# Moving a fold's first copy and addition into the list of woven jobs, and starting a unit's accumulating transfer ahead of its other half

## The chip, the cores and the metric

The kernel runs on one core of a Trainium2 chip. Its engines work in parallel, each on its own row of instructions: PE (TensorE, matrix products), DVE (VectorE), ACT (ScalarE), POOL (GpSimd) and SP (SyncE, which issues most transfers). The metric is the device time of one execution in microseconds (us), lower is better; the time before is the median of 3 runs, 2228.59 us (2227.19 to 2228.78).

## The reference

A decoder layer over 256 tokens of width 2048, all in float32: a half SwiGLU feed-forward (called f1 in the kernel), two gated token mixers (retention and windowed attention), a mixing projection, a second half feed-forward (f2) and a gated embedding, with a layer norm after each. Cut to what the change touches:

```python
def swiglu(x, w_gu, w_down):
    g, u = jnp.split(x @ w_gu, 2, axis=-1)
    return (jax.nn.silu(g) * u) @ w_down
...
h = layer_norm(alpha * h + 0.5 * swiglu(h, w_ffn1_gu[i], w_ffn1_down[i]), ln_g[i, 0], ln_b[i, 0])
...
rq, rk, rv, rg, aq, ak, av, gate_r, gate_a = jnp.split(h @ w_in[i], SPLIT_POINTS, axis=-1)
...
ret_branch = (jax.nn.silu(rg) * ro) @ w_ret_out[i]
...
mixed = (jax.nn.sigmoid(gate_r) * ret_branch + jax.nn.sigmoid(gate_a) * att_branch) @ w_mix_out[i]
...
h = layer_norm(alpha * h + 0.5 * swiglu(h, w_ffn2_gu[i], w_ffn2_down[i]), ln_g[i, 2], ln_b[i, 2])
```

The hidden width of the feed-forwards is 5632, so each has a gate/up product (2048 to 2 x 5632) and a down product (5632 to 2048).

## The kernel before, in words

**Split products.** A float32 weight tile w is split into a high part (a cast, ACT) and a low part w - high (a subtraction, DVE). PE makes three products for each pair of parts: lines L510, L511 and L512. Weights come in chunks of 512 KB, loaded by SP (L127), and are named by use: rf_gu is a raw chunk, hf_gu its high part, lf_gu its low part.

**Units.** The order of the weights is a plan, a list of units that are taken one after another. A `Single` is one chunk: cast L162 on ACT, subtraction L164 on DVE. A `Seven` holds two chunks and trades eight block products for seven (Strassen's way, in Winograd's form): DVE forms sums of blocks (L279, L280, L285, L289), ACT casts (L277, L278, L284, L293), DVE subtracts (L287, L294, L296, L298). A unit of kind "F" has a `Single` for one half and, for the other half, a pair `Folding` and `Folded`, which take the low part off DVE: ACT writes the rounded -raw into the low tile (L181), POOL issues a transfer that adds the raw chunk to it (L182), so that raw minus its rounding is left, and `Folded` casts the high part (L198). `fold_at` (L201) puts the `Folding` into the plan so many units ahead as `FOLD_AHEAD` says: 34 units of time for the first gate/up (f1_gu), 12 for the down products, 0 for the second gate/up (f2_gu).

**Buffers.** All these chunks and parts share a ring of 46 buffers of one size, which `slot` hands out in the order in which the program asks. `fill` loads from the plan and makes units as room allows; `done` frees a unit's room and calls `fill`, so the next unit's weights are made (`make_next`) while PE works on others.

**Stages and folds.** A gate/up has 11 stages, 0 to 10, one for each group of columns over the whole depth; stages 1 to 10 run as a `block` and end in a fold, named after the feed-forward and the stage (f12 is the fold of stage 2 of the first, f210 that of stage 10 of the second). Sums that only `Seven` units share stand in four extra banks, p1, p6, p7 and q5 (tiles f12s, mr0s and so on, after the block's name). When the last `Seven` of a block is done, its seven products run in the order p1, q5, p6, p7 and the rest, and `fold` combines the banks. `seven_common` does what all folds share: e = copy of p1 (ACT, L634), w0 = e + p6 (DVE, L635), w1 = w0 + p7 (L637), z = q5 - w (L639). The first two were issued at once, the others put into `woven`, a list of jobs: each call of `weave()` issues the next one, and the making of weights calls it between its own instructions. `idle` is an empty job. After the common part, a gate/up stage adds its own banks (L1105 to L1108, on f2g and f2u, f1g and f1u; a product at L1101), turns the result (ACT L227, a transposing transfer by SP, L231, ACT L238) and a mixer's block its two (L1669 to L1672). There are 28 folds: ten in each gate/up, two in each down product (f1d, f2d), two at the gates (ga0, ga1) and two at the retention output (mr0, mr1).

**Mixers.** Behind a fold of mr0 or mr1, DVE multiplies with the gates (sig, L1711) and adds (L1712), ACT writes the halves of the words (wmx, L227), SP turns them (mmx, L231), ACT joins (mixr, L238) and casts (mixt, L113), DVE subtracts (L114), and then the mixing projection can use it. The weights of the retention output (rw_ret, hw_ret, lw_ret) are made between these.

DVE, ACT and SP each take their instructions in the order in which they are written; that order, not a scheduler, decides what waits behind what.

Of the kernel before, what the change touches and what calls it, by code (L numbers as in the profile page):

```python
# [13 lines left out]
ALU = mybir.AluOpType  # L14
# [56 lines left out]
def layer(ctx: ExitStack, tc: tile.TileContext, io):  # L71
    nc = tc.nc
    sync, act, dve, pool, pe = nc.sync, nc.scalar, nc.vector, nc.gpsimd, nc.tensor
# [8 lines left out]
    def bank(name):  # L82
        return psum.tile([P, 512], F32, tag="ps", name=name)
# [4 lines left out]
    def slot(shape, dt, name):  # L88
        return slots.tile(shape, dt, tag="slot", name=name)
# [6 lines left out]
    plan = []  # L96
# [104 lines left out]
    def fold_at(ahead, key):  # L201

        begun = Folding(key)
        at, time = len(plan), 0
        while at > 0 and time < ahead:
            at -= 1
            time += plan[at].time
        if ahead and any(isinstance(u, Seven) for u in plan[at - 12 : at + 1]):
            while not isinstance(plan[at], Seven):
                at -= 1  # L210
        plan.insert(at, begun)
        plan.append(Folded(begun))

    class Turn:
# [92 lines left out]
    def weave_all():  # L307
        while woven:
            woven.pop(0)()
# [84 lines left out]
    def fill(must=False):  # L394

        while True:
            queued = sum(u.time for u in ready)
            left = room["slots"] - room["used"]
            wanted = must and not ready or not room["quiet"] and queued < room["ahead"]
            if loaded and wanted and loaded[0].makes <= left:  # L400
                make_next()
                continue
            first = loaded[0] if loaded else plan[0] if plan else None
            queued += sum(u.time for u in loaded)
            if plan and queued < room["far"] and plan[0].loads + first.makes <= left:
                u = plan.pop(0)
                u.load()
                room["used"] += u.loads
                loaded.append(u)
                continue  # L410
            return
# [9 lines left out]
    def take(key):  # L421
        while not ready:
            fill(True)
        u = ready.pop(0)
        assert u.key == key, (u.key, key)
        return u

    def done(u):
        room["used"] -= u.keeps
        fill()  # L430
        room["woven"] = room["woven"] + 1 if woven else 0
        if room["woven"] > 2:
            weave_all()
# [9 lines left out]
    idle = lambda: None  # L443

    def run_side(n=1):
        for _ in range(n):
            if side:
                side.pop(0)()
        for jobs in (slow, lazy):
            if jobs and next(jobs[0], "end") == "end":  # L450
                jobs.pop(0)
# [62 lines left out]
    def half_of(a, t):  # L514
        return tuple(x[:, t * P : (t + 1) * P] for x in a)

    def tokens_chunk(chunk, k0, lhs, sums, ts, kks=(0, 1)):
        for kk in kks:
            for t in ts:
                sums[t].add(half_of(lhs(k0 + kk), t), chunk.columns(kk))  # L520
# [11 lines left out]
    def block_units(units, keys):  # L532

        for kind, p in units:
            if kind == "P":
                plan.extend(Single(keys(n, p)) for n in range(2))
            elif kind == "F":
                plan.append(Single(keys(0, p)))
                fold_at(FOLD_AHEAD[keys(1, p)[0]], keys(1, p))
            else:  # L540
                plan.append((Seven if kind == "S" else Prepared)(keys(0, p), keys(1, p)))

    def block(name, units, keys, lhs, forms, sums, fold, before=None):


        sevens = [p for kind, p in units if kind in "SD"]
        extra = []
        for j, (kind, p) in enumerate(units):
            if before is not None:
                before(j)  # L550
            if kind in "PF":
                for n in range(2):
                    u = take(keys(n, p))
                    tokens_chunk(u.chunk, 2 * p, lhs, [sums[t][n] for t in range(2)], (0, 1))
                    done(u)
                    run_side()
                continue
            u = take(keys(0, p))
            weave_all()
            if not extra:  # L560
                extra = [Sum(bank(f"{name}s{j}"), len(sevens)) for j in range(4)]
            p1, p6, p7, q5 = extra
            a11, a12 = (half_of(lhs(2 * p + e), 0) for e in range(2))
            a22 = half_of(lhs(2 * p + 1), 1)
            f5, f6, f7, f3 = forms(p)
            q2, q3, q4 = sums[0][0], sums[0][1], sums[1][0]
            steps = [
                (p1, a11, u.b11), (q2, a12, u.b21), (q3, f3, u.b22), (q5, f5, u.t1),
                (p7, f7, u.t3), (p6, f6, u.t2), (q4, a22, u.t4),
            ]  # L570
            if p == sevens[-1]:
                steps = [steps[j] for j in (0, 3, 5, 4, 1, 2, 6)]
            for to, left, right in steps:
                to.add(left, right)
            done(u)
            run_side()
            if p == sevens[-1]:
                fold(p1.ap, p6.ap, p7.ap, q5.ap)

    def forms_sums(full):  # L580

# [49 lines left out]
    def seven_common(p1, p6, p7, q5):  # L631

        e, w, z = (slot([P, 2, 512], F32, n) for n in ("eve", "evw", "evz"))
        act.copy(e[:, 0], p1)  # L634
        dve.tensor_tensor(w[:, 0], e[:, 0], p6, ALU.add)  # L635
        woven.extend((
            lambda: dve.tensor_tensor(w[:, 1], w[:, 0], p7, ALU.add),  # L637
            idle,
            lambda: dve.tensor_tensor(z, q5[:, None, :].broadcast_to([P, 2, 512]), w, ALU.subtract),  # L639
        ))  # L640
        return e, w, z
# [423 lines left out]
    def ffn(name, i, ht, norm, keep, residual, keepers, away):  # L1065
# [60 lines left out]
        for j in range(KF // 4):  # L1126
# [22 lines left out]
            def before(u, j=j, offset=KD // 2 - len(units)):  # L1149
# [19 lines left out]
                if j == KF // 4 - 1 and u in (4, 6):  # L1169
                    convert(u // 2 - 2)  # L1170

            block(f"{name}{j}", units, gu_keys(name, j), rhs, forms, sums, lambda *a: got.extend(seven_common(*a)), before)
            if got:
                weave_all()
# [25 lines left out]
        def fold(b):  # L1200
            def f(*a):
                e, w, z = seven_common(*a)

                def scaled(x, v):
                    dve.scalar_tensor_tensor(x, x, 2.0 * ALPHA, v, ALU.mult, ALU.add)

                woven.extend((
                    lambda: scaled(y[2 * b][:, 0], e[:, 0]),
                    lambda: scaled(y[2 * b][:, 1], w[:, 1]),
                    lambda: scaled(y[2 * b + 1], z),  # L1210
                ))
            return f
# [25 lines left out]
        pn = [banks(f"{name}d{n}") for n in range(2)]  # L1238
        sums = [[Sum(pn[n][t], n_of[0][t, n]) for n in range(2)] for t in range(2)]
        block(f"{name}d0", first, down_keys(name, 0), lhs, forms, sums, fold(0), before_unit)  # L1240
        weave_all()
        for n in range(2):
# [21 lines left out]
        pt_ = [banks(f"{name}e{t}") for t in range(2)]  # L1264
        sums = [[Sum(pt_[t][n], n_of[1][t, n]) for n in range(2)] for t in range(2)]
        block(f"{name}d1", second, down_keys(name, 1), lhs, forms, sums, fold(1), before_unit)
        weave_all()
        slots_for_weights(27, last_ahead, last_ahead + 24)
# [72 lines left out]
    def mixers(ht, norm, residual, keepers, away):  # L1341
# [320 lines left out]
        def mixer_block(name, units, keys, lhs):  # L1662

            ps = [banks(name + w) for w in "ab"]
            got = []
            block(name, units, keys, lhs, forms, block_sums(ps, units, KD), lambda *a: got.extend(seven_common(*a)))
            weave_all()
            e, w, z = got
            dve.tensor_tensor(e[:, 0], e[:, 0], ps[0][0], ALU.add)  # L1669
            dve.tensor_tensor(e[:, 1], w[:, 1], ps[1][0], ALU.add)  # L1670
            for t in range(2):
                dve.tensor_tensor(z[:, t], z[:, t], ps[t][1], ALU.add)  # L1672
            return [e, z]
# [400 lines left out]
```

## Time and profile before

| | us |
|---|---|
| median of 3 runs | 2228.59 |
| profiled execution, its time | 2229.62 |
| its span in the profile | 2227.6 |
| DVE busy in it | 2011.8 |
| ACT busy in it | 1451.7 |
| transfers from HBM over the span | 490.20 MB, 235 GB/s |

The profiled execution is 1.03 us slower than the median. A row of the timeline reads: start, duration, engine, line, operation, output<-inputs, shape, count, and in brackets the idle time of the engine before it and what released it. The windows give for stretches of the span the busy time of each engine, then the granted clock of PE as a share (1.00 is all), the share of the transfer engines and GB/s. A window is cut at the end of p1, so it holds one stage from fold to fold. "x3" in a row are three instructions back to back.

### The profile page before, as it was taken

The numbers are of one execution on the slowest core, as the hardware profiler recorded it, in microseconds if no ns is written. First come the engines' busy times: TensorE is split into PE (matmuls) and PEld (weight loads), VectorE is DVE, ScalarE is ACT, GpSimd is POOL, SyncE is SP. The second block draws the span as 40 slices with busy tenths as digits, with TensorE's granted clock in tenths as the row PEclk, the third lists the DMA queues.
The fourth block names the chain that finished last, engine by engine and source line by source line (L and its number), as shares of the span: only waits on it lengthen the run. The fifth ranks groups of instructions, "written<-read, shape, count | busy, mean of one in ns | idle before, by whom it ended". The sixth has DMA issues, their size and how long they took to land.

```text
span 2227.6 us, 29127 instructions
## 1 busy us (share of the span) xinstructions
PE 2215.5 (99%) x10116; PEld 1832.7 (82%) x10116; DVE 2011.8 (90%) x2656; ACT 1451.7 (65%) x1691; POOL 48.4 (2%) x62
## 2 busy tenths in 40 slices
PE   9999999999999999999999999999999999999998
PEld 7788888888888888888788888888888877888887
DVE  5999999999988889889999888779999999899887
ACT  5877777777565545557866567466767678665553
POOL 0000000000000000000000000000000000000000
PEclk9999999999999999999999999999999999999999
DMA  9979889977686889846976578888899898777771
GB/s 315 259 227 264 249 241 263 255 239 235 225 301 238 296 280 331 274 171 228 293 232 232 174 216 323 306 302 269 290 313 312 292 265 260 215 242 234 283 290 69
DMA packets 303339, 573.91 MB, mean 258 GB/s; under 512 B 98764, under 2 KB 103756, under 8 KB 303192
## 3 DMA queue, kind: packets, MB, share of 16 engines
q1 hardware_dynamic: 293576, 541.70, 72.5%
q0 software_dynamic: 7632, 27.79, 6.7%
q10 hardware_dynamic: 1984, 2.58, 0.4%
q8 instruction: 79, 1.29, 0.2%
q14 instruction: 68, 0.56, 0.1%
HBM read 490.20 MB, written 33.55 MB: 235 GB/s over the span
## 4 chain that ended last, share of the span: by engine, by line
PE 92%; DMA 3%; DVE 3%; issue 2%; ACT 1%; SPq 0%; ACTq 0%; POOLq 0%; DVEq 0%
PE rqk L461 3%; PE f1g L512 3%; PE f1g L510 3%; PE f1g L511 3%; PE f2g L510 2%; PE f2g L511 2%; PE f2g L512 2%; PE f1u L512 2%; PE f1u L510 2%; PE f1u L511 2%; PE f2u L512 2%; PE f2u L510 2%; PE f2u L511 2%; PE aqk L461 2%; PE f2d L512 1%
## 5 line engine op out<-in xcount | busy, mean ns | idle before, releaser
L164 DVE TENSOR_TENSOR lw_in_f<-rw_in_f,hw_in_f 128x1024 fp32r<-128x1024 f32 x132 | 158.2, 1219 | 14.5 <-ACT hw_in_f L162 14.3
L164 DVE TENSOR_TENSOR lf_gu<-rf_gu,hf_gu 128x1024 fp32r<-128x1024 f32 x123 | 145.1, 1219 | 22.8 <-ACT hf_gu L162 22.1
L162 ACT CAST hf_gu<-rf_gu 128x1024 fp32r<-128x1024 f32 x123 | 123.3, 1048 | 29.7 <-DMA rf_gu<-in_f_gu 27.8
L293 ACT CAST hvf_gu<-vf_gu 128x1024 fp32r<-128x1024 f32 x83 | 87.5, 1055 | 76.5 <-DVE vf_gu L289 62.6
L284 ACT CAST huf_gu<-uf_gu 128x1024 fp32r<-128x1024 f32 x83 | 87.3, 1052 | 76.6 <-DVE uf_gu L280 69.3
L162 ACT CAST hw_in_f<-rw_in_f 128x1024 fp32r<-128x1024 f32 x132 | 132.5, 1049 | 6.9 <-DMA rw_in_f<-in_w_in_f 4.2
L164 DVE TENSOR_TENSOR lf_down<-rf_down,hf_down 128x1024 fp32r<-128x1024 f32 x96 | 115.6, 1220 | 20.5 <-ACT hf_down L162 16.3
L162 ACT CAST hf_down<-rf_down 128x1024 fp32r<-128x1024 f32 x96 | 98.5, 1049 | 27.3 <-DMA rf_down<-in_f_down 11.8
L287 DVE TENSOR_TENSOR lf_gu<-rf_gu,hf_gu 128x1024 fp32r<-128x1024 f32 x83 | 101.1, 1218 | 0.0
L298 DVE TENSOR_TENSOR lvf_gu<-vf_gu,hvf_gu 128x1024 fp32r<-128x1024 f32 x83 | 101.1, 1218 | 0.0
L296 DVE TENSOR_TENSOR luf_gu<-uf_gu,huf_gu 128x1024 fp32r<-128x1024 f32 x83 | 101.1, 1218 | 0.0
L277 ACT CAST hf_gu<-rf_gu 128x1024 fp32r<-128x1024 f32 x83 | 86.8, 1046 | 8.4 <-DMA rf_gu<-in_f_gu 8.4
L512 PE MATMUL f1g<-lf_gu,xt 128*128 128x512 f32 x223 | 87.1, 391 | 1.1 <-DVE lf_gu L164 1.1
L510 PE MATMUL f1g<-hf_gu,xt 128*128 128x512 f32 x223 | 87.0, 390 | 0.1
L511 PE MATMUL f1g<-hf_gu,xt 128*128 128x512 f32 x223 | 86.8, 389 | 0.0
L510 PE MATMUL f2g<-hf_gu,ht 128*128 128x512 f32 x196 | 76.4, 390 | 0.0
L512 PE MATMUL f2g<-lf_gu,ht 128*128 128x512 f32 x196 | 76.3, 389 | 0.0
L511 PE MATMUL f2g<-hf_gu,ht 128*128 128x512 f32 x196 | 76.3, 389 | 0.0
L512 PE MATMUL f1u<-lf_gu,xt 128*128 128x512 f32 x180 | 70.1, 390 | 0.0
L510 PE MATMUL f1u<-hf_gu,xt 128*128 128x512 f32 x180 | 70.1, 390 | 0.0
L511 PE MATMUL f1u<-hf_gu,xt 128*128 128x512 f32 x180 | 70.0, 389 | 0.0
L182 POOL DMA_DIRECT2D lf_gu<-rf_gu x37 | 32.2, 871 | 1636.9 <-DMA rf_gu<-in_f_gu 1105.6
(1568 smaller groups left out, 7220.3 us busy)
## 6 DMA issues: line engine op xcount, KB each, us to landing
rf_gu<-in_f_gu SPq DMA_DIRECT2D x362, 512.0 KB
rf_down<-in_f_down SPq DMA_DIRECT2D x176, 512.0 KB
rw_in_f<-in_w_in_f SPq DMA_DIRECT2D x148, 512.0 KB
lf_gu<-rf_gu POOLq DMA_DIRECT2D x37, 512.0 KB, 8.5
rw_rv<-in_w_rv SPq DMA_DIRECT2D x32, 512.0 KB
rw_ret<-in_w_ret SPq DMA_DIRECT2D x32, 512.0 KB
rw_mix<-in_w_mix SPq DMA_DIRECT2D x32, 512.0 KB
rw_pg<-in_w_pg SPq DMA_DIRECT2D x32, 512.0 KB
```

What stands on the lines that cost most here:

```text
L162: act.copy(c.hi, c.raw)
L164: dve.tensor_tensor(c.lo, c.raw, c.hi, ALU.subtract)
L277: act.copy(a.hi, a.raw)
L284: act.copy(uh, u)
L287: dve.tensor_tensor(a.lo, a.raw, a.hi, ALU.subtract)
L293: act.copy(vh, v)
L296: dve.tensor_tensor(ul, u, uh, ALU.subtract)
L298: dve.tensor_tensor(vl, v, vh, ALU.subtract)
L461: pe.matmul(ps[f], hi[:, kk, f * P : (f + 1) * P], rhs(k), start=k == 0, stop=k == n_k - 1,)
L510: pe.matmul(o, al, bh, start=first, stop=False)
L511: pe.matmul(o, ah, bh, start=False, stop=False)
L512: pe.matmul(o, ah, bl, start=False, stop=self.left == 0)
```

## The change

Three edits. In `fold_at`, where nothing is said to be ahead (f2_gu only), the `Folding` goes before the last unit of the plan, the `Single` of the same pair, and no longer after it. In `block`, the fold is called before the last unit's `done` and `run_side`. In `seven_common`, the copy and w0 are no longer issued at once but become the first job of `woven`, followed by an empty one; the other jobs move back by two. So the copy and w0 are issued in the first `weave()` of the next making, and their lines become one (L635; w1 is L637, z is L639).

```diff
-        plan.insert(at, begun)
+        plan.insert(at if ahead else len(plan) - 1, begun)
         plan.append(Folded(begun))
...
             for to, left, right in steps:
                 to.add(left, right)
+            if p == sevens[-1]:
+                fold(p1.ap, p6.ap, p7.ap, q5.ap)
             done(u)
             run_side()
-            if p == sevens[-1]:
-                fold(p1.ap, p6.ap, p7.ap, q5.ap)
...
         e, w, z = (slot([P, 2, 512], F32, n) for n in ("eve", "evw", "evz"))
-        act.copy(e[:, 0], p1)
-        dve.tensor_tensor(w[:, 0], e[:, 0], p6, ALU.add)
         woven.extend((
+            lambda: (act.copy(e[:, 0], p1), dve.tensor_tensor(w[:, 0], e[:, 0], p6, ALU.add)),
+            idle,
             lambda: dve.tensor_tensor(w[:, 1], w[:, 0], p7, ALU.add),
             idle,
             lambda: dve.tensor_tensor(z, q5[:, None, :].broadcast_to([P, 2, 512]), w, ALU.subtract),
```

The rows below are instructions as they stand on an engine; numbers behind a name are the buffer's count. First place: DVE at the fold f12 (end of stage 2 of the first gate/up, bank f12s), where the making of the next `Single`'s low part and the sums of the next `Seven` follow.

```order
 L164 TENSOR_TENSOR lf_gu_0_7_1110<-rf_gu_0_7_1011,hf_gu_0_7_1109 128x1024
 L164 TENSOR_TENSOR lf_gu_1_7_1135<-rf_gu_1_7_1057,hf_gu_1_7_1134 128x1024
-L164 TENSOR_TENSOR lf_gu_0_5_1166<-rf_gu_0_5_1095,hf_gu_0_5_1165 128x1024
 L635 TENSOR_TENSOR evw<-eve,f12s_985 128x512
+L164 TENSOR_TENSOR lf_gu_0_5_1169<-rf_gu_0_5_1095,hf_gu_0_5_1168 128x1024
 L279 TENSOR_TENSOR uf_gu_0_0_1195<-rf_gu_1_0_1142 128x512
 L280 TENSOR_TENSOR uf_gu_0_0_1195<-rf_gu_0_0_1140,rf_gu_1_0_1142 128x512
```

One subtraction, lf_gu_0_5, now stands behind w0 (L635) instead of ahead of it. Second place: DVE at the fold mr0 in the mixers (bank mr0s), up to z.

```order
 L164 TENSOR_TENSOR lw_ret_2_7_11889<-rw_ret_2_7_11850,hw_ret_2_7_11888 128x1024
-L164 TENSOR_TENSOR lw_ret_4_2_11914<-rw_ret_4_2_11852,hw_ret_4_2_11913 128x1024
-L164 TENSOR_TENSOR lw_ret_6_2_11918<-rw_ret_6_2_11854,hw_ret_6_2_11917 128x1024
 L635 TENSOR_TENSOR evw<-eve,mr0s_11641 128x512
-L279 TENSOR_TENSOR uw_ret_4_0_11942<-rw_ret_6_0_11874 128x512
-L280 TENSOR_TENSOR uw_ret_4_0_11942<-rw_ret_4_0_11872,rw_ret_6_0_11874 128x512
+L164 TENSOR_TENSOR lw_ret_4_2_11917<-rw_ret_4_2_11852,hw_ret_4_2_11916 128x1024
 L637 TENSOR_TENSOR evw<-evw,mr0s_11642 128x512
-L285 TENSOR_TENSOR vw_ret_4_0_11943<-rw_ret_4_0_11872,uw_ret_4_0_11942 128x512
-L287 TENSOR_TENSOR lw_ret_4_0_11946<-rw_ret_4_0_11872,hw_ret_4_0_11945 128x1024
+L164 TENSOR_TENSOR lw_ret_6_2_11923<-rw_ret_6_2_11854,hw_ret_6_2_11922 128x1024
```

Two subtractions, lw_ret_4_2 and lw_ret_6_2, go behind w0, with w1 (L637) between them; the sums of the next `Seven` (L279 on) follow after the second. At mr1 one subtraction goes behind w0 and one behind w1 in the same way, and on ACT the copy stands between the two casts that belong to them instead of behind both. Third place: ACT in the last stage of the second gate/up, at its last unit "F" (hf_gu and lf_gu ending in 0_6 and 1_6 are the two halves' parts).

```order
 L293 CAST hvf_gu_0_1_16884<-vf_gu_0_1_16868 128x1024
-L162 CAST hf_gu_0_6_16907<-rf_gu_0_6_16839 128x1024
-L181 ACTIVATE lf_gu_1_6_16942<-rf_gu_1_6_16853 128x1024
-L198 CAST hf_gu_1_6_16945<-rf_gu_1_6_16853 128x1024
+L181 ACTIVATE lf_gu_1_6_16907<-rf_gu_1_6_16839 128x1024
+L162 CAST hf_gu_0_6_16910<-rf_gu_0_6_16841 128x1024
+L198 CAST hf_gu_1_6_16945<-rf_gu_1_6_16839 128x1024
```

The start of the low part (L181) goes ahead of the other half's cast (L162); on SP the two loads rf_gu_0_6 and rf_gu_1_6 change places in the same way. There are ten such units in the second gate/up.

## The prediction

> **What bounds the kernel now.** I read the page first (span, busy time), then the waits of PE (TensorE), then the windows cut at the folds (the ends of the accumulations that the change touches), then the timelines around single folds.
>
> ```profile
> span 2227.6 us, 29127 instructions
> PE 2215.5 (99%) x10116; PEld 1832.7 (82%) x10116; DVE 2011.8 (90%) x2656; ACT 1451.7 (65%) x1691; POOL 48.4 (2%) x62
> ```
>
> PE is busy 2215.5 of 2227.6 us. So 12.1 us are left, and work on other engines counts only where it stops PE. PE's waits:
>
> ```profile
> PE f2u L512 <- DMA lf_gu<-rf_gu: 1.5, 2, 0.9
> PE f1g L512 <- DVE lf_gu L164: 1.1, 2, 0.5
> PE mr1a L512 <- DVE lw_ret L164: 0.5, 1, 0.5
> PE f29s L510 <- DVE evz L1108: 0.3, 1, 0.3
> ```
>
> The columns are total, times, longest. Three of these lie at places that the change touches: f2u (accumulating transfers of the second gate/up), mr1a (weights behind a fold), f29s (a bank that DVE empties). Matmuls start 0.23 us apart while each row lasts 0.39, so a pause that PE's rows show is a little shorter than the real one.
>
> Now the stages, cut where p1, the first bank of a fold, ends (columns: window, length, then busy PE, PEld, DVE, ACT, POOL):
>
> ```profile
> 125.50:165.60 40.10, 40.10 (x178) 33.21 (x178) 39.04 (x50) 29.29 (x33) 2.62 (x3) 1.00 0.75 219
> 206.50:246.60 40.10, 40.10 (x178) 33.20 (x178) 40.10 (x51) 29.76 (x33) 2.59 (x3) 1.00 0.84 244
> 287.70:327.80 40.10, 40.10 (x179) 33.20 (x178) 39.45 (x50) 29.29 (x32) 2.59 (x3) 1.00 0.76 226
> 1563.30:1602.70 39.40, 39.40 (x176) 32.62 (x175) 39.40 (x49) 27.11 (x30) 0.00 (x0) 1.00 0.83 283
> ```
>
> DVE (VectorE), not only PE, is full here: 40.10 of 40.10. In 125.50:165.60 it idles 1.06, in 287.70:327.80 it idles 0.65, each time in one wait that stands before the line that moves (below). How closely PE follows is seen at the ends of these stages:
>
> ```profile
> 165.25 1.21 DVE L298 TENSOR_TENSOR lvf_gu<-vf_gu,hvf_gu 128x1024 fp32r<-128x1024 f32 x1
> 246.46 1.22 DVE L298 TENSOR_TENSOR lvf_gu<-vf_gu,hvf_gu 128x1024 fp32r<-128x1024 f32 x1
> 327.18 1.22 DVE L298 TENSOR_TENSOR lvf_gu<-vf_gu,hvf_gu 128x1024 fp32r<-128x1024 f32 x1
> 166.57 0.45 PE L512 MATMUL f13s<-lvf_gu,f1fm 128*128 128x512 f32 x1
> 247.73 0.50 PE L512 MATMUL f15s<-lvf_gu,f1fm 128*128 128x512 f32 x1
> 328.80 0.39 PE L512 MATMUL f17s<-lvf_gu,f1fm 128*128 128x512 f32 x1
> ```
>
> The last weights are ready at 166.46, 247.68 and 328.40 and used at 166.57, 247.73 and 328.80: slack 0.11, 0.05 (the hand-off itself) and 0.40 us. A delay of DVE in these stages reaches PE almost whole.
>
> **The change, part by part.** No instruction is added or removed; all is order.
>
> *1. Copy and first addition into the list.* The addition w0 (L635) needs p1 and p6, and p6 ends later. It now stands ahead of one or two subtractions (L164) that are ready. DVE works in order, so when DVE is ahead of PE those queue behind a wait, and so does the next making of weights (L279 on). First gate/up stage:
>
> ```profile
> 122.76 3.49 DVE L164 TENSOR_TENSOR lf_gu<-rf_gu,hf_gu 128x1024 fp32r<-128x1024 f32 x3
> 127.31 0.69 DVE L635 TENSOR_TENSOR evw<-eve,f12s 128x512 f32<-128x512 f32 x1 [1.06 <-ACT lf_gu L181]
> 127.91 0.68 DVE L279 TENSOR_TENSOR uf_gu<-rf_gu 128x512 f32<-128x512 f32 x1
> 208.52 0.68 DVE L635 TENSOR_TENSOR evw<-eve,f14s 128x512 f32<-128x512 f32 x1
> 209.12 0.68 DVE L279 TENSOR_TENSOR uf_gu<-rf_gu 128x512 f32<-128x512 f32 x1
> 289.18 0.69 DVE L635 TENSOR_TENSOR evw<-eve,f16s 128x512 f32<-128x512 f32 x1 [0.65 <-PE f16s L512]
> 289.83 0.69 DVE L279 TENSOR_TENSOR uf_gu<-rf_gu 128x512 f32<-128x512 f32 x1
> ```
>
> At f16 w0 starts when PE lets it: 289.18, 1.48 after the cut at 287.70. Taken as the earliest w0 of every fold, this gives 126.98 (f12), 207.98 (f14). (At f12 it started 0.33 later than that, held by something of its tile's buffer; the tile gets another buffer now, so I drop that.) A subtraction takes (3.49-1.22)/2 = 1.135, an addition 0.60. So L279 comes at 126.98+0.60+1.135 = 128.71 instead of 127.91 (+0.80), at 207.98+1.735 = 209.71 instead of 209.12 (+0.59), and at 289.18+1.735 = 290.92 instead of 289.83 (+1.09). Less the slacks (0.05 being no slack): 0.80-0.06 = 0.74, 0.59, 1.09-0.35 = 0.74, together **+2.1**. These stages have no other DVE idle to absorb it; bounds 0 (if DVE catches up in ways the rows don't show) and +2.5 (no slack at all). In the stages between, and from f17 on, DVE is behind PE or waits for loads, and w0 finds its banks full: 0.
>
> *2. The same at the mixers' folds mr0 and mr1.*
>
> ```profile
> 1298.77 1.23 DVE L164 TENSOR_TENSOR lw_ret<-rw_ret,hw_ret 128x1024 fp32r<-128x1024 f32 x1 [0.63 <-ACT hw_ret L162]
> 1300.90 1.23 DVE L164 TENSOR_TENSOR lw_ret<-rw_ret,hw_ret 128x1024 fp32r<-128x1024 f32 x1 [0.90 <-ACT hw_ret L162]
> 1302.40 0.69 DVE L635 TENSOR_TENSOR evw<-eve,mr0s 128x512 f32<-128x512 f32 x1 [0.28 <-PE mr0s L512]
> 1311.17 0.68 DVE L1669 TENSOR_TENSOR eve<-eve,mr0a 128x512 f32<-128x512 f32 x1
> 1331.56 2.56 ACT L238 COPY mixr<-mmx 128x1024 uint16<-128x1024 uint16 x2 [0.63 <-DMA mmx<-wmx]
> 1335.20 1.99 ACT L162 CAST hw_ret<-rw_ret 128x1024 fp32r<-128x1024 f32 x2
> 1336.28 2.36 DVE L164 TENSOR_TENSOR lw_ret<-rw_ret,hw_ret 128x1024 fp32r<-128x1024 f32 x2 [0.18 <-ACT hw_ret L162]
> 1338.56 0.68 DVE L635 TENSOR_TENSOR evw<-eve,mr1s 128x512 f32<-128x512 f32 x1
> 1322.30 9.19 DMA mmx<-wmx
> ```
>
> Here w0 already waits for PE (0.28), until 1302.40, and both subtractions, done at 1298.77 and 1300.90 in the waiting time, now come after it: 2 x 1.135 = 2.27 later for L1669 and what follows. The chain of waits goes on from there without a break: DVE's sums, the transposing transfer mmx at 1322.30 (last row; 9.19 us), ACT's copies at 1331.56, casts at 1335.20, the subtraction at 1336.28, PE's wait at mr1a. All of it moves by +2.27, less nothing. At mr1 the copy (0.49) goes behind the first of the two casts, which ends at 1336.19, and w0 ahead of the subtraction that PE waits for: w0 at 1336.80, subtraction at 1337.40 instead of 1336.28, about +1.05. PE stands at that weight already, so the two add: **+3.3**. Bounds: +1.1 (the transfer's start is set by something else than DVE) and +3.8 (the 0.5 us of wait that PE has at mr1a now doesn't count against it).
>
> *3. The same in the second gate/up.*
>
> ```profile
> 1560.63 4.62 DVE L164 TENSOR_TENSOR lf_gu<-rf_gu,hf_gu 128x1024 fp32r<-128x1024 f32 x4
> 1565.17 0.68 DVE L635 TENSOR_TENSOR evw<-eve,f22s 128x512 f32<-128x512 f32 x1
> 1579.26 0.67 DVE L1108 TENSOR_TENSOR evz<-evz,f2u 128x512 f32<-128x512 f32 x1
> ```
>
> At f22 two of the four subtractions fall behind w0. DVE is through the other two at 1560.63+2x1.135 = 1562.90 and waits until 1563.30+1.48 = 1564.78: +1.88 for what follows. Weights are more than 3 us early there, so what matters is the bank that L1108 empties at 1579.93 and PE takes 1.6 us later: +0.3 to +0.4. f21 has the same +1.9 but no bank so near; f23 to f27 have 2 to 5 us of slack. f28 adds 0.2 before the full stage 9. Together **+0.6**, bounds 0 and +1.5 (the delays of f21, f24 and f29 reach PE by some tenths each).
>
> *4. The accumulating transfers one unit sooner.*
>
> ```profile
> 1867.39 1.04 ACT L162 CAST hf_gu<-rf_gu 128x1024 fp32r<-128x1024 f32 x1
> 1868.34 1.05 ACT L181 ACTIVATE lf_gu<-rf_gu 128x1024 fp32r<-128x1024 f32 x1
> 1869.75 0.86 POOL L182 DMA_DIRECT2D lf_gu<-rf_gu  x1 [17.54 <-ACT lf_gu L181]
> 1869.75 9.03 DMA lf_gu<-rf_gu
> ```
>
> L181 now comes ahead of the cast of its unit and its load ahead of the other half's load on SP's queue; nothing else on SP moves. ACT is free of waits here, so L181 is 0.95 sooner, or less if its load lands last: 0.3 to 0.95. The transfer of 9.03 us ends as much sooner, and PE's wait in stage 10 (the 0.9 among f2u's 1.5) shrinks by it: **-0.7**. In stage 9 the other 0.6 goes too, but at the stage's end PE meets DVE's last weights, as in 247.73 above, so it is worth 0. The cast of the unit comes 0.95 later, but DVE reaches its subtraction no sooner than before. Bounds -1.5 and +0.3 (DVE waits for the late cast).
>
> The 37 starts of these transfers on POOL (GpSimd) take this:
>
> ```profile
> L182 POOL DMA_DIRECT2D lf_gu<-rf_gu x37: 859/862/1020, 34.9 to 1869.8; - x37
> ```
>
> The Trainium skill (SBUF — State Buffer, A bandwidth-pool intuition that's wrong) has a case that speaks against part 4: while DVE holds the shared port, descriptors of a transfer issued from POOL can't be written, 620 ns becoming 3100 ns. The trace doesn't show it: 862 in the median and 1020 at most, beside a DVE that is full. By that rule the moved start could lose 2.5 us instead of gaining 0.7.
>
> *Earlier tiles.* The three tiles of the fold are taken earlier, so later loads get other buffers, some released up to 2 us later. Most of these loads wait for the queue and not for a buffer; I count 0, bounds 0 and +3 (the 2 us whole at one stage without slack, half at another).
>
> **Sum**: 2.1+3.3+0.6-0.7 = +5.3 us on the profiled execution, which took 2229.62 (2.0 around its span). The median of the runs shown, 2228.59, is 1.0 below it, so **2233.9**.
>
> **The rivals.**
> A. *What the change removes and no more.* If the waits at mr0, mr1 and f12 to f16 do not lengthen, f2u's 1.5, mr1a's 0.5 and f29s's 0.3 go, and with the start-to-start correction about 3.5: 2225.1. It decides where the banks are full before DVE comes to w0. The row at 208.52 speaks for it, where w0 waits for nothing; the 0.28 and 0.65 us of waits for PE before w0 in the rows above speak against it.
> B. *One of the two large terms is hidden:* the mixers (transfer not set by DVE) or the first stage: +5.3-2.1 or +5.3-2.2, 2231.9.
> C. *More than the sum:* loads into other buffers come late and DVE, full in most gate/up stages, can't make it up: +3 to +4 more, 2237.5.
> D. *POOL held at the moved start:* two subtractions of DVE, 2 x 1.135 = 2.27 us, less the 0.95 gained, make stages 9 and 10 each 1.3 later where the sum has 0.7 gained: 5.3+0.7+2.6 = +8.6, 2237.2. The 1020 ns above speak against it. This is the rule of the Trainium skill's page on SBUF, weighed in part 4.
> E. *The order changes and PE sees none of it:* 2228.6.
>
> **How the numbers follow.** Chances: forecast 0.46 (2231.5 to 2236.5 by its bounds), A 0.12, B 0.24, C 0.13, D 0.02, E 0.03. The range 2226.5 to 2238 leaves out most of A's lower part, and the top of C. A measurement tells 0.2% (4.5 us) from no change: faster is below 2224.1, slower above 2233.05. Slower has two thirds of the forecast, C and D: 0.47. Faster has the far half of A: 0.06. The rest is same: 0.47. The forecast stands just outside that bound.
>
> **What would show it.** Right: w0 preceded by a wait for PE of about 1.9 at f12, 1.3 at f14; L1669 2.3 later after mr0; PE's wait at mr1a 3 us longer; at 166, 247 and 328 PE pauses of 0.6 to 0.7 on L298. Part 4: POOL's start in stage 10 0.3 to 0.95 sooner against the cast L277 behind it, f2u's 1.5 near 0.5. Wrong: a total of PE's idle time under 12 us, mmx issued no later after mr0's p1, or pauses of PE on DMA at places that have none now (C).

## The result, and the profile after

The changed kernel takes 2232.92 us in the median of 13 runs (2230.79 to 2235.39), the kernel before 2227.31 us on the same chips (2225.64 to 2228.78). The ratio is 1.0024, 95% interval 1.0016 to 1.0033: slower by 0.24%, or 5.6 us. The forecast was 2233.9 against 2228.59, which is a ratio of 1.0024 too. The profiled execution took 2230.79 us.

The page of the profile after, span and busy time:

```profile
span 2229.0 us, 29129 instructions
PE 2215.6 (99%) x10116; PEld 1833.3 (82%) x10116; DVE 2009.9 (90%) x2656; ACT 1453.0 (65%) x1691; POOL 48.3 (2%) x62
```

The two spans differ by 1.4 us only, where the medians differ by 5.6. Most of the reason stands at the start. The copy at the fold f12 is a good clock for it, since it can't start before PE has filled its bank (timeline of ACT, before and then after; the row after names nothing that released it):

```profile
125.57 0.59 ACT L634 COPY eve<-f12s 128x512 f32<-128x512 f32 x1 [0.66 <-PE f12s L512]
```

```profile
122.01 0.59 ACT L635 COPY eve<-f12s 128x512 f32<-128x512 f32 x1 [1.80 <-issue]
```

The execution after reached f12 3.56 us sooner. Two more profiles of the kernel before (last two experiments) show that this start varies from run to run. So two single spans can hide a change of this size, and I compare stretches between the same instructions. PE's waits after (total, times, longest):

```profile
PE mr1a L512 <- DVE lw_ret L164: 2.4, 2, 1.6
...
PE f29s L512 <- DVE luf_gu L296: 0.7, 1, 0.7
PE f29s L510 <- DVE eve L1105: 0.3, 1, 0.3
PE f23s L510 <- DVE evz L1108: 0.3, 1, 0.3
PE f29s L510 <- DVE evz L1108: 0.3, 1, 0.3
```

mr1a went from 0.5 to 2.4, f23s is new, f2u's 1.5 is gone, and f29s has new waits of 0.7 for L296 and 0.3 for L1105. In the first gate/up, DVE around the folds f12, f14 and f16:

```profile
123.40 0.69 DVE L635 TENSOR_TENSOR evw<-eve,f12s 128x512 f32<-128x512 f32 x1 [2.03 <-PE f12s L512]
...
125.14 0.68 DVE L279 TENSOR_TENSOR uf_gu<-rf_gu 128x512 f32<-128x512 f32 x1
...
205.18 0.69 DVE L635 TENSOR_TENSOR evw<-eve,f14s 128x512 f32<-128x512 f32 x1 [1.08 <-ACT eve L635]
...
206.92 0.68 DVE L279 TENSOR_TENSOR uf_gu<-rf_gu 128x512 f32<-128x512 f32 x1
...
286.99 0.69 DVE L635 TENSOR_TENSOR evw<-eve,f16s 128x512 f32<-128x512 f32 x1 [1.71 <-PE f16s L512]
...
288.73 0.68 DVE L279 TENSOR_TENSOR uf_gu<-rf_gu 128x512 f32<-128x512 f32 x1
```

DVE now idles 2.03, 1.08 and 1.71 us before w0 (before: 1.06, 0 and 0.65), while the subtraction that stood ahead of w0 before now stands behind it. (The row at f14 names ACT's copy, but that ended at 204.35; the last product of p6 starts at 204.70 and its row ends at 205.09, so there too it is more likely PE that w0 waits for.) A stage later, PE at the last weights:

```profile
162.12 0.39 PE L511 MATMUL f13s<-huf_gu,f1fm 128*128 128x512 f32 x1
162.62 0.50 PE L512 MATMUL f13s<-luf_gu,f1fm 128*128 128x512 f32 x1
...
163.76 0.50 PE L512 MATMUL f13s<-lvf_gu,f1fm 128*128 128x512 f32 x1 [0.18 <-DVE lvf_gu L298]
...
245.53 0.50 PE L512 MATMUL f15s<-lvf_gu,f1fm 128*128 128x512 f32 x1 [0.17 <-DVE lvf_gu L298]
...
327.35 0.50 PE L512 MATMUL f17s<-lvf_gu,f1fm 128*128 128x512 f32 x1 [0.17 <-DVE lvf_gu L298]
```

The waits that the rows show are small (0.17), and 162.12 to 162.62 shows none at all, though matmuls that run freely start 0.23 apart: 0.27 is lost there. Only start-to-start times carry such pauses. From f12's copy to the first of these places PE takes 163.76-122.01 = 41.75 us (before 166.57-125.57 = 41.00), from there to the second 81.77 (before 247.73-166.57 = 81.16), to the third 81.82 (before 81.07): +0.75, +0.61, +0.75.

At the mixers, first the copy at mr0 and PE's wait in the timeline before:

```profile
1300.97 0.59 ACT L634 COPY eve<-mr0s 128x512 f32<-128x512 f32 x1
...
1337.56 0.50 PE L512 MATMUL mr1a<-lw_ret,rett 128*128 128x512 f32 x1 [0.53 <-DVE lw_ret L164]
```

Then the same and DVE between them, after (timelines of ACT, DVE and PE):

```profile
1299.61 0.59 ACT L635 COPY eve<-mr0s 128x512 f32<-128x512 f32 x1 [2.42 <-PE mr0s L512]
...
1301.04 0.69 DVE L635 TENSOR_TENSOR evw<-eve,mr0s 128x512 f32<-128x512 f32 x1 [4.10 <-PE mr0s L512]
...
1312.06 0.68 DVE L1669 TENSOR_TENSOR eve<-eve,mr0a 128x512 f32<-128x512 f32 x1
...
1337.42 0.69 DVE L635 TENSOR_TENSOR evw<-eve,mr1s 128x512 f32<-128x512 f32 x1 [0.65 <-ACT eve L635]
1338.03 1.22 DVE L164 TENSOR_TENSOR lw_ret<-rw_ret,hw_ret 128x1024 fp32r<-128x1024 f32 x1
...
1339.30 0.51 PE L512 MATMUL mr1a<-lw_ret,rett 128*128 128x512 f32 x1 [1.60 <-DVE lw_ret L164]
```

And the transposing transfer in the chain of waits after:

```profile
1323.18 8.97 DMA mmx<-wmx
```

Counted from the copy at mr0, L1669 comes after 12.45 us (before 10.20, +2.25), the transfer after 23.57 (before 21.33, +2.24), and the weight at mr1a after 39.69 (before 36.59, **+3.10**). DVE's idle 4.10 us before w0 holds what were two subtractions.

The parts of the span, all from rows shown here and in the prediction:

| stretch | before | after | difference |
|---|---|---|---|
| start to the copy at f12 | 125.57 | 122.01 | -3.56 |
| to the last weight at f17s | 203.23 | 205.34 | +2.11 |
| to the copy at mr0 | 972.17 | 972.26 | +0.09 |
| to the weight at mr1a | 36.59 | 39.69 | +3.10 |
| to the end of the span | 890.04 | 889.70 | -0.34 |

Without the start that is +5.0, beside 5.6 in the medians. How far each of these stretches varies from one run of a program to the next is shown with the last experiments.

### The profile page after: what moved, and what is told of

It reads as the page before. It is cut to its first block, busy times and chain, and to the rows that moved or that the text cites. A ratio compares the mean times of both kernels' runs of the same rounds, so it can differ in the third digit from the quotient of the medians.

```text
span 2229.0 us, 29129 instructions
## 1 busy us (share of the span) xinstructions
PE 2215.6 (99%) x10116; PEld 1833.3 (82%) x10116; DVE 2009.9 (90%) x2656; ACT 1453.0 (65%) x1691; POOL 48.3 (2%) x62
## 4 chain that ended last, share of the span: by engine, by line
PE 82%; DVE 4%; issue 1%; DMA 1%; ACT 0%; ACTq 0%; SPq 0%; DVEq 0%
PE rqk L461 3%; PE f2g L510 2%; PE f2g L511 2%; PE f2g L512 2%; PE f2u L510 2%; PE f2u L511 2%; PE f2u L512 2%; PE aqk L461 2%; PE f2e L512 1%; PE f2e L511 1%; PE f2d L512 1%; PE f1e L511 1%; PE f1d L512 1%; PE f1d L511 1%; PE f2d L511 1%; PE f1e L512 1%
## 5 line engine op out<-in xcount | busy, mean ns | idle before, releaser
L162 ACT CAST hw_in_f<-rw_in_f 128x1024 fp32r<-128x1024 f32 x132 | 132.6, 1048 | 6.7 <-DMA rw_in_f<-in_w_in_f 3.9
L162 ACT CAST hf_gu<-rf_gu 128x1024 fp32r<-128x1024 f32 x123 | 124.1, 1047 | 17.8 <-DMA rf_gu<-in_f_gu 17.8
L162 ACT CAST hf_down<-rf_down 128x1024 fp32r<-128x1024 f32 x96 | 98.6, 1049 | 29.5 <-DMA rf_down<-in_f_down 12.7
L298 DVE TENSOR_TENSOR lvf_gu<-vf_gu,hvf_gu 128x1024 fp32r<-128x1024 f32 x83 | 101.3, 1221 | 0.0
L296 DVE TENSOR_TENSOR luf_gu<-uf_gu,huf_gu 128x1024 fp32r<-128x1024 f32 x83 | 101.3, 1221 | 0.0
```

The costliest lines, as they stand in the source:

```text
L162: act.copy(c.hi, c.raw)
L296: dve.tensor_tensor(ul, u, uh, ALU.subtract)
L298: dve.tensor_tensor(vl, v, vh, ALU.subtract)
```

## The experiments

Each run was compared with the kernel before on the same chip; a figure in us is the difference of the two medians, and the interval is that of the ratio.

**The Folding's new place alone.**

```diff
-        plan.insert(at, begun)
+        plan.insert(at if ahead else len(plan) - 1, begun)
```

> Of the change only the Folding's place in the plan (part 4 of the prediction); copy and w0 as before. Theory (all of the loss comes from w0 waiting ahead of ready work on DVE): f1 and the mixers as before (PE's wait at mr1a 0.5), f2u's wait of 1.5 on the accumulating transfers gone, of which stage 9's part returns as a wait for DVE's last weights: 0.4 to 1.3 us less than before, most likely -1.0, within noise of no change. Rival (the changed order of loads and casts costs part of the loss): +1 us or more, with waits of PE in stages 4 to 10 of f2 that before doesn't have.

Measured: 2226.47 against 2226.44 us, ratio 0.9999 (0.9990 to 1.0008). A gain of 1 us is inside that interval and can't be told from it. In its profile f2u waits for no transfer, and PE's waits have this row, which no profile of the kernel before has:

```profile
PE f29s L512 <- DVE luf_gu L296: 0.7, 1, 0.7
```

The rival is not borne out: the profile has no other new wait in the second gate/up, though the interval alone would still allow +1 us. What the edit gains in stage 9 (0.75 us by start times) is given back at that stage's end (0.83), where PE, sooner there, waits for DVE.

**The list alone.** The change without the line above.

> Of the change only the copy and w0 in the list; the Folding's place as before. Theory: the whole loss and a little more, since the gain of the accumulating transfers is missing: +5.5 to +6.5 us, with PE waiting for L298 at the ends of f1's stages 3, 5 and 7 by 0.6 each, 2.4 in all at mr1a, 0.3 to 0.5 at f23s, and f2u's 1.5 still there. Rival (the loss hangs on both edits together): under +4.

Measured: 2232.41 against 2226.44 us, +6.0, ratio 1.0024 (1.0015 to 1.0033). mr1a has its 2.4 as expected, f23s 0.2 where 0.3 to 0.5 was expected, and from the copy at f12 to the last weight at f17s PE takes 205.28 us, as long as in the changed kernel (205.34). f2u is there:

```profile
PE f2u L512 <- DMA lf_gu<-rf_gu: 2.0, 2, 1.6
```

So the list carries the whole loss. In this profile 1.6 us behind the weight at mr1a is something else, told at the end (the clock).

**The whole change, with the mixers' two folds mr0 and mr1 as before.** A test of the block's name chooses between the fold ahead of `done`, through the list, and the fold behind `run_side`, issued at once:

```diff
-            if p == sevens[-1]:
+            early = not name.startswith("mr")
+            if p == sevens[-1] and early:
                 fold(p1.ap, p6.ap, p7.ap, q5.ap)
             done(u)
             run_side()
+            if p == sevens[-1] and not early:
+                at_once.append(1)
+                fold(p1.ap, p6.ap, p7.ap, q5.ap)
```

> The whole change, but at mr0 and mr1 the copy and w0 are issued as before. Theory: 3.1 us less than the changed kernel, so +2.0 to +2.8 over before; between the folds mr0 and mr1 and from mr1 to f21 PE takes as long as before. Rival (PE's later waits swallow it): as slow as the changed kernel, +5.

Measured: 2229.29 against 2226.44 us, +2.9, ratio 1.0012 (1.0004 to 1.0021), just above the +2.0 to +2.8 expected, where the whole change has +5.6. The wait at mr1a is back to what it was before:

```profile
PE mr1a L512 <- DVE lw_ret L164: 0.5, 1, 0.5
```

About half of the loss belongs to two of 28 folds.

**The list, but with the fold called where it was.** The first and the third edit without the second, so that w0 moves later and not earlier.

> The Folding's new place, and the copy and w0 in the list, but the fold still called after the last unit's done and run_side, so that the first job comes in the making of the next Seven, behind its first two sums: w0 moves later where the change moves it earlier. Theory: DVE's waits before w0 (1.1 at f12, 0.6 at f16, 0.3 at mr0) are filled by the two sums, L1669 after mr0 comes 0.3 sooner, and no stage of f1 is longer than before: -1.0 to -1.5 us against before. Rival (being in the list is itself what costs, by later banks or the pairing of the jobs): +1 or more.

Measured: 2234.95 against 2226.44 us, +8.5 in the medians (ratio 1.0032, 1.0019 to 1.0044), the slowest of all. A clear miss: the rival's sign was right. f1 and mr1a show no wait that the kernel before doesn't have in one of its profiles, but in the second gate/up PE waits for banks and weights:

```profile
PE f28s L512 <- DVE luf_gu L296: 1.3, 1, 1.3
...
PE f27s L510 <- DVE evz L1107: 0.6, 1, 0.6
```

L1107 empties a bank and stands in the same list as w0, at its end. A later w0 moves the list's end back, and with it the bank. I had counted the wait before w0 as lost time and not what hangs on the list's end. That this is the cause at f27 is argued from these rows; no run takes it apart. By start times PE loses 3.9 us at the folds f25 to f28, of some 6 us in this profile; where the rest goes was not found.

**The change at mr0 alone, and at mr1 alone.** As in the mixers' run, with `early = name == "mr0"` and `"mr1"`, and the Folding's place as before.

> Before, with the change's copy and w0 in the list at the fold mr0 alone. Theory (two subtractions of 1.135 us each lose the time that DVE spent waiting for PE before w0, and the transposing transfer passes the delay on): L1669 2.25 later after mr0, from mr0 to the next fold PE takes 1.0 to 1.1 us more, from there to f21 another 1.1 to 1.3, PE's wait at mr1a 1.6 to 1.7 in all; +2.2 us. Rival (the transfer's start is set by something else, so that the delay is lost in DVE's 2.6 us of waiting before mixt): +1.1 at most.

> Before, with the change's copy and w0 in the list at the fold mr1 alone. Theory (PE stands at the weight that the copy of 0.49 and w0 of 0.60 now precede): nothing up to mr1, PE's wait at mr1a 1.5 where before had 0.5; +1.07 us. With the run on mr0 alone it adds up to the 3.1 us that the whole change loses here. Rival (the two hide each other): +1.07 here, but under 2.6 for the sum of the two.

Measured: at mr0 2228.56 against 2226.64 us, +1.9 (ratio 1.0008, 0.9999 to 1.0016, so by the medians alone not clear of no change), at mr1 2228.47, +1.8 (1.0011, 1.0002 to 1.0020). The sum of 3.8 has the size of the 2.8 that separate the mixers' run from the whole change, as far as such intervals tell. The profiles are sharper. The copy at mr0 and the weight at mr1a, with the list at mr0 alone:

```profile
1298.26 0.59 ACT L638 COPY eve<-mr0s 128x512 f32<-128x512 f32 x1 [2.30 <-PE mr0s L512]
...
1336.88 0.50 PE L512 MATMUL mr1a<-lw_ret,rett 128*128 128x512 f32 x1 [0.53 <-DVE lw_ret L164]
```

And with the list at mr1 alone:

```profile
1297.84 0.58 ACT L638 COPY eve<-mr0s 128x512 f32<-128x512 f32 x1
...
1335.94 0.53 PE L512 MATMUL mr1a<-lw_ret,rett 128*128 128x512 f32 x1 [1.60 <-DVE lw_ret L164]
```

That is 38.62 and 38.10 us. The same stretch took 36.59 in the first profile before and 37.2 in two more (below), so at 37.0 in the mean the two lengthen it by 1.6 and 1.1. The whole change's 39.69 is 2.7 more. They add up (2.7), if only just above the 2.6 under which the rival had put the sum. The row of 1.60 speaks more plainly against the rival that they hide each other: PE's pause at this weight is 1.60 with the list at mr1 alone and 1.60 with both, where it was 0.53. With the list at mr0 alone this pause is not longer, since PE is late there itself, from an earlier wait at mr1a and one at mr1s; its waits at mr1a are 1.3 in all, where 1.6 to 1.7 was expected.

**The whole change, with w0 one job later.** One subtraction stands ahead of it again.

```diff
         woven.extend((
-            lambda: (act.copy(e[:, 0], p1), dve.tensor_tensor(w[:, 0], e[:, 0], p6, ALU.add)),
             idle,
+            lambda: (act.copy(e[:, 0], p1), dve.tensor_tensor(w[:, 0], e[:, 0], p6, ALU.add)),
             lambda: dve.tensor_tensor(w[:, 1], w[:, 0], p7, ALU.add),
```

> The whole change, but with the empty job ahead of the copy and w0 and not behind them, so that one subtraction of the next making stands ahead of w0 again; w1 and z at the same places in the list as in the changed kernel. Theory (only the ready subtractions behind w0 cost): no wait of PE for L298 at the ends of f1's stages 3, 5 and 7 beyond 0.1, none at f23s, at the mixers 1.1 us instead of 3.1; +1 from that, -1 from the accumulating transfers, so within 0.6 us of before. Rival (the earlier call of the fold or the earlier tiles cost): the same 2.2 us in f1 as the changed kernel.

Measured: 2226.41 against 2226.64 us, ratio 1.0000 (0.9991 to 1.0009). PE's waits at f13s, f17s and f23s are gone, and at the mixers:

```profile
1298.00 0.59 ACT L636 COPY eve<-mr0s 128x512 f32<-128x512 f32 x1 [2.48 <-PE mr0s L512]
...
1335.85 0.50 PE L512 MATMUL mr1a<-lw_ret,rett 128*128 128x512 f32 x1 [0.53 <-DVE lw_ret L164]
```

That is 37.85 us, 0.8 over the mean of before, for one subtraction of 1.135. This is the plainest test: the call of the fold and the tiles are the changed kernel's, one step in the order differs, and the 5.6 us are gone. The early call and the early tiles cost nothing that these medians can tell (the interval reaches 2 us to each side); the place of the copy and w0 costs. A wait of 0.2 at f15s stays, which the kernel before has too in one of three profiles.

**The same kernels once more, for their profiles.**

> The kernel before once more, for one more profile. Theory: the start (to the end of f11's first bank at 83.84 us in the first profile, 81.1 to 82.4 in the profiles of five other kernels that are the same up to there) varies from run to run by up to 3 us and is no part of the change; the waits of f2u on the accumulating transfers are there again within 0.5 of 1.5. Rival (the start depends on the change, or f2u's waits on the run): 83.8 again, or f2u's waits under 0.5 or over 2.5.

> The kernel before a third time, for its profile: theory: f2u's waits between 0.8 and 2, mr1a 0.5, the end of f11's first bank between 81 and 84 us. Rival (the first profile's 1.5 of f2u was an outlier): f2u under 0.5.

The copy at f12 in the timeline of the kernel before, second profile and third, and then f2u's row in PE's waits of the second and the third:

```profile
122.89 0.59 ACT L634 COPY eve<-f12s 128x512 f32<-128x512 f32 x1 [0.64 <-PE f12s L512]
```

```profile
124.46 0.59 ACT L634 COPY eve<-f12s 128x512 f32<-128x512 f32 x1 [0.65 <-PE f12s L512]
```

```profile
PE f2u L512 <- DMA lf_gu<-rf_gu: 1.0, 2, 0.8
```

```profile
PE f2u L512 <- DMA lf_gu<-rf_gu: 0.5, 1, 0.5
```

The start varies by 2.7 us over three runs of one program, and the list at mr1 alone, which is the kernel before up to that point, has 122.28; so nothing shows the -3.56 to be an effect of the change. f2u's waits vary too, 1.5, 1.0 and 0.5, more than I expected of the third (0.8 to 2). None of the second and third profile's lies in stage 10, where the first has its 0.9.

The other stretches, in the three profiles of the kernel before and the two of the changed one:

| stretch | before | changed |
|---|---|---|
| copy at f12 to the last weight at f17s | 203.2, 203.3, 203.5 | 205.3, 205.3 |
| to the copy at mr0 | 972.2, 972.3, 972.1 | 972.3, 972.3 |
| to the weight at mr1a | 36.6, 37.2, 37.2 | 39.7, 40.4 |
| to the end of the span | 890.0, 889.0, 888.8 | 889.7, 891.8 |

Against the mean of before, the first gate/up is 1.9 to 2.0 longer in both, the mixers 2.7 and 3.4, and the end 0.4 and 2.5; 1.6 of that 2.5 are the clock (told at the end). The first profile before, from which the prediction was worked out, is the shortest of the three at the mixers and the longest at the end.

> The changed kernel once more, for one more profile. Theory: every pause that hangs on w0's place comes back at its place and size (0.6 each at the ends of f1's stages 3, 5 and 7, 2.4 in all at mr1a, 0.4 at f23s), and f2u waits for no accumulating transfer. Open: after the pause of 1.77 us at mr1a the granted clock fell for 3 us in two of the three kernels that have that pause (ten matmuls at 0.43 instead of 0.23), not in the changed one: if that is chance of the run, it may show here. Rival (f2u's waits gone by chance, since they vary between 1.0 and 2.0 in kernels without the Folding's new place): f2u waits of 0.4 or more here.

> The run on mr1 alone once more, for one more profile. Theory: PE's wait at mr1a is 1.6 again; from mr1 to f21 1.07 us more than before if the clock does not fall after it, 2.7 more if it falls again. f2u waits 1.0 to 2.0. Rival (the clock's fall belongs to this program): it falls again at the same matmuls, here and in every run.

A row of PE's waits in the changed kernel's second profile, and one in that of the list at mr1 alone:

```profile
PE mr1a L512 <- DVE lw_ret L164: 2.4, 2, 1.6
```

```profile
PE f2u L512 <- DMA lf_gu<-rf_gu: 2.1, 3, 1.2
```

The changed kernel shows 2.4 at mr1a again, its 0.3 at f23s, and no wait of f2u. With the list at mr1 alone the wait at mr1a is 1.6 again, as expected, and f2u's 2.1 is a little over the 1.0 to 2.0 expected. So f2u never waits in the five profiles that have the Folding's new place and the fold called early or w0 at its old place, and waits 0.5 to 2.1 in the seven with its old place: in stage 9 in all seven, in stage 10 in three of them. In the run with the late list, which has the new place, it waits 0.6, in stage 10.

No version beats the kernel before by what can be measured: the two that come out level are the Folding's place alone and w0 one job later.

## Why the prediction was right, step by step

**f1, forecast +2.1: measured +2.11**, as 0.75, 0.61 and 0.75 against 0.74, 0.59 and 0.74 (1.9 to 2.0 against the mean of three profiles before, in both of the changed kernel). DVE was full there and the slack of PE was known from rows, so each delay of L279 reached PE. The later start of w0 could be read in advance from one fold (f16) in which w0 already waited for PE alone. Wrong in a detail: the pauses were to be seen on L298; they are spread over L296 and L298.

**Mixers, forecast +3.3: measured +3.10** (2.7 and 3.4 against the mean of three profiles before). Against the first profile the first half was exact, L1669 +2.25 against 2.27; the transfer started 2.24 later and took 8.97 instead of 9.19, so that it passed on 2.0. The second half was 1.07, from 0.53 to 1.60 in the rows at mr1a; the prediction's own rows give 1.12 (1337.40 less 1336.28) where it wrote 1.05. PE's own waits at mr1a grew by 1.9 in the rows (0.5 to 2.4), where 3 was forecast as the sign; the rest of the 3.10 lies in smaller pauses before, at mr1s above all. That the two add is borne out by the runs at mr0 and mr1 alone. But the exactness of the first half is luck. In the second and the third profile before, the instruction behind w0 waits for a load, as in this row of the second:

```profile
1301.42 0.69 DVE L279 TENSOR_TENSOR uw_ret<-rw_ret 128x512 f32<-128x512 f32 x1 [0.75 <-DMA rw_ret<-in_w_ret]
```

There L1669 comes 11.0 us after the copy and not 10.2, and the changed kernel's 12.45 is only 1.4 to 1.5 later: the two subtractions fill that wait. The prediction took one profile's order of events for the program's.

**Second gate/up, forecast +0.6:** f23s waits for L1108, 0.3 by its row, at the place and with the engine that was named. By start times PE takes 0.5 to 0.6 longer from the fold f22 to f23s in the four profiles that have the list and the early call in this gate/up. The runs with w0 one job later and with the Folding alone don't show it.

**Accumulating transfers, forecast -0.7: not shown to be an effect of the change.** I let the transfer of 9.03 us in stage 10 start 0.3 to 0.95 sooner. In the profile after, POOL's start in stage 10 (timeline) and the time to landing (the tile's view of this stage) are

```profile
1872.56 0.86 POOL L182 DMA_DIRECT2D lf_gu<-rf_gu  x1 [18.32 <-ACT lf_gu L181]
```

```profile
DMA to landing us min/median/max: 7.0/7.0/7.0
```

PE's last weight at the fold f29 stands at 1845.64 before and at 1848.63 after:

```profile
1845.64 0.50 PE L512 MATMUL f29s<-lvf_gu,f2f2h 128*128 128x512 f32 x1 [0.17 <-DVE lvf_gu L298]
```

```profile
1848.63 0.50 PE L512 MATMUL f29s<-lvf_gu,f2f2h 128*128 128x512 f32 x1 [0.16 <-DVE lvf_gu L298]
```

From there the start comes after 23.93 us (before 24.11): only 0.18 sooner. The rest came from a transfer that took 7.0 and not 9.03, and that varies by itself: in the third profile of the kernel before it took 6.0 (the tile's view of this stage), and PE's matmul that had waited 0.93 in the first profile shows no wait (timeline):

```profile
DMA to landing us min/median/max: 6.0/6.0/6.0
```

```profile
1877.68 0.39 PE L512 MATMUL f2u<-lf_gu,ht 128*128 128x512 f32 x1
```

In the second it took 7.6, without a wait either. With the Folding's old place PE waits in stage 10 in the three profiles whose transfer took 9.0 us or more, and in none of the four with 7.9 or less. So the wait of 0.9 was chance of the profile that the prediction was read from. What the new place does remove is stage 9's wait, in every profile; it was worth nothing, as forecast, and the row of 0.7 at L296 shows where it is handed back.

**How much of the agreement is luck.** The two large terms came at the places and through the waits that were named, and near the sizes; that is no luck. The gain of 0.7 is not shown to be the change's, and without it the sum would have been +6.0. Without the start and without the clock's 1.6, the two profiles of the changed kernel are 5.1 and 6.4 over the mean of before, so the runs can't tell 5.3 from 6.0. The clock was not in the sum at all, and how many of the 13 runs have its 1.6 is not known. That 5.3 came so near to 5.6 is in part chance.

**Rivals.** A, the waits that the change removes and no more, falls: the banks are not full before DVE comes to w0. B, one of the large terms hidden, falls with the stretches of f1 and of the mixers, both longer in both profiles of the changed kernel. C, more than the sum, falls: between f17s and mr0 after takes 0.09 us longer, through all loads in other buffers. D, POOL held at the start, falls: the row above has 0.86, as before, and no start in the profile after took more than 1.02.

## What to carry to other kernels

Moving a job that waits for another engine ahead of ready work on its own engine turns idle time that was filled into idle time that isn't, and the price is the ready work that now stands behind it. That does not mean the later the better: with the late list the same job stands behind two more sums, and the loss was the largest of all, so look also at what hangs on the job's end. Find the price from one place in the trace where the job already waits for the other engine alone, and charge it only where the stage has no slack. To see 0.2%, compare the stretches between the same instructions of two profiles, after two or three profiles of one kernel have told which stretches vary by themselves. Read a forecast from more than one profile too: the wait of 0.9 in stage 10 and the missing wait of 0.75 at mr0 were each one run's own.

## What the runs showed of the hardware that was not expected

After the pause of 1.6 us at mr1a (1.8 by start times), PE's granted clock fell in some runs. The windows of the list alone, then of the changed kernel (window, length, busy PE, PEld, DVE, ACT and POOL, granted clock):

```profile
1341.00:1345.00 4.00, 4.00 (x12) 3.11 (x11) 4.00 (x4) 4.00 (x6) 0.00 (x0) 0.60 1.03 413
```

```profile
1341.00:1345.00 4.00, 4.00 (x19) 3.31 (x18) 4.00 (x4) 4.00 (x6) 0.00 (x0) 1.00 1.02 411
```

In the timeline of PE, of the list alone, matmuls start 0.43 us apart instead of 0.23:

```profile
1341.07 0.63 PE L511 MATMUL mr1b<-hw_ret,rett 128*128 128x512 f32 x1
1341.50 0.63 PE L512 MATMUL mr1b<-lw_ret,rett 128*128 128x512 f32 x1
```

Eight or so matmuls at 0.2 more are 1.6 us. It is seen in three of five profiles with that pause: the list alone, mr1 alone, and the second profile of the changed kernel, but not in that kernel's first profile or the second one of mr1 alone. In the eight profiles without that pause no matmul behind this weight is slow. So whether the clock falls hangs on the run and not on the program alone, and here the pause of 1.6 us cost its own length once more in three runs of five. The Trainium skill (TensorE: Matmul & The Clock Gate, Part 1: The HAM clock gate) gives 426.7 ns from start to start for a matmul of 512 columns while the clock is throttled; the 0.43 here agrees. The same section puts throttling after an idle window of about 3.4 us, one that runs freely; the pause here was shorter than that, and the clock fell all the same in three runs.
